# Modulation steps grouped in runs, narrow matmuls gathered around them, and a rearranged entry into the MLP, in a one-core decoder step

## The chip, the cores and the metric

The kernel runs on one core of one Trainium2 chip. The metric is the device time of one execution in microseconds (us), as the median of several runs. The core has a matrix engine (PE, with its weight loads shown as PEld), a vector engine (DVE), an activation engine (ACT), GpSimd (POOL) and a synchronisation engine (SP), which here issues most of the DMA transfers. Each engine executes its own instructions in the order in which they were written to it.

## The reference

One layer of a hybrid decoder runs on a prompt of 256 tokens and on 8 samples of one token each, in fp32, with a model width of 2048:

```python
mod = silu(c) @ w_ada + b_ada                 # 6 x 2048 per sequence
sh1, sc1, gt1, sh2, sc2, gt2 = split(mod, 6)
h = rmsnorm(x, g_pre_mix) * (1 + sc1) + sh1
z = h @ w_in                                  # inputs of three mixers, three gates
y_a = spatial_gating(...)                     # A
y_b = gated_linear_recurrence(...)            # B, 8 heads of 128 x 128
y_c = gated_linear_recurrence(...)            # C, 4 heads of 128 x 256
merged = sum(sigmoid(z_gate[n]) * (y[n] @ w_branch[n]) for n in range(3))
x = x + gt1 * rmsnorm(merged @ w_out, g_post_mix)
h2 = rmsnorm(x, g_pre_mlp) * (1 + sc2) + sh2
x = x + gt2 * rmsnorm(square(relu(h2 @ w_mlp_up)) @ w_mlp_down, g_post_mlp)
```

The recurrent states of prompt and samples, and the normalised rows of mixer A, are outputs as well. `mod` is the **modulation**: six rounds of 2048 values for the prompt and each of the 8 samples.

## The kernel before, in words

**Main work.** All activations stand transposed, 264 columns wide (256 prompt tokens and 8 samples). Every weight tile of 128 x 128 is multiplied three times, with the high and low parts of weights and activations: high x high (L567), high x low (L568), low x high (L569). I call these the main matmuls; there are 13872 of them. A *granule* (`granule`) is 24 of them on one weight block, in two halves of 12. SP loads the raw weights into four buffers, up to five granules ahead (`LOAD_AHEAD`). ACT casts each half to its high part (`whi`, L112), and DVE subtracts to get the low part (`wlo`, L109). Both have six buffers (`SPLIT_BUFS`): the split of a half therefore waits until PE has used the half that stands six before it.

**Stages.** A start with norms and the first two modulation rounds; the mixer inputs (`begin`); the three branches, each with gate and projection matmuls per block of 256 outputs; the output projection `w_out` in eight blocks (m = 0 to 7); a short stretch that I call the *MLP front*; the MLP with eight blocks of up and down projections; a tail.

**Background work.** The mixers are Python generators in the queues `bg` (mixers) and `bs` (samples). After each granule `background` advances them by a rate (`RATES`), and what they emit is thus written between the main matmuls. Three kinds of their PE work use only 32 columns or rows of the array, and I call them **narrow**: levels of the chunked attention (L593, 32 columns), sample reads of the recurrent state (L600) and modulation steps (L307). `slot` emits them together, two levels at most.

**Modulation.** `ada_round` computes rounds 2, 3 and 4 during the branches. A round has 16 steps. A step is four matmuls with 512 moving columns, shown as eight records in the trace. Its two weight tiles `araw` are loaded as soon as the step before it has been issued (L300, two buffers), and steps stand at least four granules apart (`ADA_GAP`). Round 5 has its weights for six steps loaded early into `b` tiles (`N_PRE` = 12 tiles at m = 2 to 5); these steps fill the MLP front, and the other ten run singly in the MLP.

**Waiting places.** `b` tiles (28 buffers) hold most intermediate blocks, and a new one waits for an old one's last reader. The narrow PSUM tiles `sm` have three buffers. In a level, DVE subtracts (L109), ACT takes exponentials (L1077), DVE multiplies twice (L103) and PE reads the result. In the samples, ACT decays the loaded states (L1012) and DVE adds the outer product with a loaded broadcast (`vbc`, L1014). Mixer B and C outputs are transposed back by L1202 and copied by ACT in L1204.

**MLP front.** After the last block of `w_out` come the norm, transposes of the last gated block into the PSUM pair `pt`, sums for the second norm, `residual(q)` (L1466, adds the branch to the residual rows on DVE) and `quad(q)` (L1479 and L1481 scale and transpose four blocks; L1486 and L1488 modulate them). `put_rows(7)` copies `pt` to rows on ACT (L1357) and DVE (L1358). The first MLP accumulators reuse the PSUM that `pt` holds.

Of the kernel before, what the change touches and what calls it, by code (L numbers as in the profile page):

```python
# [15 lines left out]
P = 128  # L16
# [20 lines left out]
RATES = ((1.7, 0.5, 0.27), (1.5, 0.5, 0.27), (1.2, 0.5, 0.27), (1.0, 0.5, 0.27))  # L37
ST_BUFS = 4
VB_BUFS = 2
N_PRE = 12  # L40
PRE_AT = (2, 3, 4, 5)
R0 = 0.3
# [6 lines left out]
FILL = 3  # L49
READY = object()  # L50
SLOT_LATE = 0.9
SLOT_WAIT = 3
# [4 lines left out]
ADA_GAP = 4  # L57
# [3 lines left out]
def hybrid_step_kernel(  # L61
# [229 lines left out]
    def ada_round(r, pre=()):  # L291

        acc = pada.tile([P, 512], F32, tag="ada", name=nm("ada"))

        def load(n):
            if n < len(pre):
                return pre[n]
            w = rawp.tile([P, 1024], F32, tag="araw", name=nm("araw"), bufs=ADA_RAW)
            c0 = r * D + n % 2 * 1024
            nc.sync.dma_start(w, w_ada[0, n // 2 * P:(n // 2 + 1) * P, c0:c0 + 1024])  # L300
            return w

        ws = [load(0), load(1)]
        yield
        for k in range(KT):
            for j in range(4):
                T.matmul(acc[32 * j:32 * j + 32, :], cT[:, k, :], ws[j // 2][:, j % 2 * 512:j % 2 * 512 + 512], start=k == 0, stop=k == KT - 1)  # L307
            ws = [load(2 * k + 2), load(2 * k + 3)] if k + 1 < KT else []
            yield
        am = ada_am(acc, 512)  # L310
        yield
        rows = ada_rows(am, 512)
        ch = slice(r * KT, (r + 1) * KT)
        add(
            mod[:, ch, :].rearrange("p (j i) c -> p i j c", i=4),
            rows[:, :, :, 0:NC],
            badaT[:, ch].rearrange("p (j i) -> p i j", i=4).unsqueeze(3).to_broadcast([P, 4, 4, NC]),
        )
        yield
# [43 lines left out]
    bg, bs, ba = Queue(), Queue(), Queue()  # L363
# [97 lines left out]

    rate = [0.0, 0.0, R0]

# [93 lines left out]
    def granule(w, k0, n, c0, width, accs, xh, xl, k, first, last):  # L557
# [3 lines left out]
        h = n // 2  # L561
        for acc0, m0 in [(acc, 2 * i) for i, acc in enumerate(accs)]:
            for j in range(n):
                for m in range(m0, min(m0 + 2, width // P)):
                    o = acc0[:, m % 2, 0:NT]
                    a, b = (p[:, j % h, m * P:(m + 1) * P] for p in parts[j // h])
                    T.matmul(o, a, xh(k + j), start=first and j == 0, stop=False)  # L567
# [3 lines left out]

    ada_at = [0]

    def ada_due():

        return ba.g and ba.owed >= 0.0 and now[0] >= ada_at[0] + ADA_GAP
# [3 lines left out]
    def slot():  # L580
# [20 lines left out]
        if ada_due():  # L601
            ada_at[0] = now[0]
            ba.step()
# [1054 lines left out]
```

## Time and profile before

| | |
|---|---|
| median of 3 runs | 1972.18 us (1970.73 to 1972.27) |
| the profiled execution's time | 1970.37 us |
| its span in the trace | 1968.6 us, so 1.8 us lie outside |
| mean granted PE clock | 0.994 |
| PE busy | 1919.0 us, 97% |
| DVE busy | 1190.3 us, 60% |
| ACT busy | 1003.6 us, 51% |
| DMA | 442.05 MB, mean 225 GB/s |

A timeline row gives the start of a group of equal instructions, its duration, engine, line, operation, tiles, shape and count. Brackets hold the engine's idle time just before it and what released it. In a table of windows, the third column group gives each engine's busy time in order PE, PEld, DVE, ACT, POOL with record counts, then the granted PE clock as a share of full speed, the DMA share and GB/s. Matmuls overlap, so their distance from start to start matters, not their duration. Line numbers here are those of the kernel before; the changed kernel has about 2 less at the helpers (L109 becomes L107) and about 40 more later (L1202 becomes L1243).

### The profile page before, as it was taken

Reading aid. Unit: us, or ns where it says so; the run is one execution under the profiler, and the core shown is the slowest. Engines: PE = TensorE matmul, PEld = TensorE weight load, DVE = VectorE, ACT = ScalarE, POOL = GpSimd, SP = SyncE. Lnnn points to the kernel's source line nnn. Section 1 sums busy time; section 2 is a strip of 40 time slices with the busy share of each in tenths; the row PEclk is TensorE's granted clock in tenths of the full one; section 3 lists DMA queues with packets and bytes.
Section 4 is the critical chain, followed back from the end, with each engine's and each line's share of the span. In section 5 each row is a group of like instructions: output and inputs, shape, how many; then the busy total and the mean of one; then the engine's idle time right before and its main releaser. Section 6 shows DMA issues by size and latency. Waiting matters only on the chain. (4 is left out here: it accounts for less than half of the span.)

```text
span 1968.6 us, 42184 instructions
## 1 busy us (share of the span) xinstructions
PE 1919.0 (97%) x17008; PEld 1821.4 (93%) x17008; DVE 1190.3 (60%) x2100; ACT 1003.6 (51%) x1818; POOL 83.9 (4%) x142
## 2 busy tenths in 40 slices
PE   6999999999989999999999999999999999999998
PEld 5889999889979999899999989999999999999997
DVE  4566667686766694555555666544555555555665
ACT  5444354655845754644444555444444445454544
POOL 1000000111001111110000000000000000000000
PEclk9999999999999999999999999999999999999999
DMA  9897697788577788678887844767565556566653
GB/s 326 303 337 249 228 302 225 228 252 269 182 240 252 217 265 295 205 251 267 271 249 214 306 141 142 227 220 232 175 182 181 181 179 182 180 181 183 182 178 103
DMA packets 339379, 442.05 MB, mean 225 GB/s; under 512 B 14930, under 2 KB 281024, under 8 KB 339184
## 3 DMA queue, kind: packets, MB, share of 16 engines
q1 hardware_dynamic: 329120, 409.62, 65.5%
q0 software_dynamic: 8992, 28.48, 4.5%
q8 instruction: 133, 2.18, 0.4%
q10 hardware_dynamic: 1072, 1.25, 0.2%
q14 instruction: 62, 0.51, 0.1%
HBM read 427.60 MB, written 11.70 MB: 223 GB/s over the span
## 5 line engine op out<-in xcount | busy, mean ns | idle before, releaser
L567 PE MATMUL mm<-b,whi 128*128 128x264 f32 x4624 | 1330.8, 288 | 10.6 <-ACT b L112 3.5
L568 PE MATMUL mm<-b,whi 128*128 128x264 f32 x4624 | 1318.4, 285 | 1.2 <-DVE b L109 1.2
L569 PE MATMUL mm<-b,wlo 128*128 128x264 f32 x4624 | 1314.3, 284 | 0.0
L109 DVE TENSOR_TENSOR wlo<-raw,whi 128x512 fp32r<-128x512 f32 x1136 | 778.0, 690 | 587.1 <-ACT whi L112 581.5
L112 ACT CAST whi<-raw 128x512 fp32r<-128x512 f32 x1136 | 695.6, 618 | 765.5 <-PE mm L568 681.7
L567 PEld LDWEIGHTS mm<-b,whi 128*128 128x128 f32 x4624 | 872.8, 189 | 70.1 <-ACT whi L112 31.7
L568 PEld LDWEIGHTS mm<-b,whi 128*128 128x128 f32 x4624 | 873.7, 189 | 1.8 <-DVE b L109 1.6
L569 PEld LDWEIGHTS mm<-b,wlo 128*128 128x128 f32 x4624 | 873.2, 189 | 0.0
L106 DVE TENSOR_TENSOR b<-b,mm 128x528 f32<-128x528 f32 (+1 forms) x137 | 95.7, 700 | 44.4 <-PE mm L569 44.4
L1014 DVE SCALAR_TENSOR_TENSOR st<-vbc,b,st 128x128 f32<-128x128 f32 (+1 forms) x96 | 33.8, 392 | 52.0 <-DMA vbc<-vs_d 43.9
L307 PE MATMUL ada<-araw,cT 128*32 128x512 f32 x464 | 63.5, 602 | 0.3 <-DMA araw<-in_w_ada_dram 0.3
L1012 ACT ACTIVATE st<-st,fs 128x128 f32<-128x128 f32 (+1 forms) x96 | 36.8, 430 | 49.3 <-DMA st<-in_state_gla_dram 27.2
L277 PE MATMUL ada<-b,cT 128*32 128x256 f32 (+1 forms) x640 | 35.3, 359 | 6.6 <-ACT b L226 5.6
L103 DVE TENSOR_TENSOR b<-b,b 128x512 f32<-128x512 f32 (+1 forms) x47 | 34.2, 744 | 4.0 <-ACT b L1129 1.4
L277 PEld LDWEIGHTS ada<-b,cT 128*32 128x32 f32 x640 | 18.3, 115 | 18.8 <-ACT b L226 5.6
L1015 POOL DMA_DIRECT2D out_dram<-st x32 | 23.5, 735 | 125.2 <-DVE st L1014 114.5
L109 DVE TENSOR_TENSOR b<-gt,b 128x528 fp32r<-128x528 f32 x32 | 22.7, 709 | 3.7 <-ACT whi L112 0.5
L109 DVE TENSOR_TENSOR b<-b 128x1024 f32<-128x1024 f32 (+1 forms) x21 | 22.4, 1068 | 2.1 <-PE sm L593 1.2
L112 ACT CAST whi<-araw 128x512 fp32r<-128x512 f32 x20 | 12.4, 621 | 21.0 <-PE mm L568 19.2
L103 DVE TENSOR_TENSOR gt<-vt 128x528 f32<-128x528 f32 x32 | 22.5, 702 | 0.9 <-ACT vt L1522 0.9
L1528 ACT ACTIVATE b<-vt 128x528 fp32r<-128x528 f32 x32 | 20.7, 647 | 1.0
L1522 ACT ACTIVATE vt<-mm 128x528 f32<-128x528 f32 x32 | 19.4, 607 | 1.0 <-PE mm L569 1.0
(338 smaller groups left out, 824.2 us busy)
## 6 DMA issues: line engine op xcount, KB each, us to landing
raw<-in_w_in_dram SPq DMA_DIRECT2D x232, 512.0 KB, 4.7
raw<-in_w_mlp_up_dram SPq DMA_DIRECT2D x128, 512.0 KB, 3.9
raw<-in_w_mlp_down_dram SPq DMA_DIRECT2D x128, 512.0 KB, 3.7
araw<-in_w_ada_dram SPq DMA_DIRECT2D x116, 512.0 KB, 5.4
b<-in_w_ada_dram SPq DMA_DIRECT2D x60, 512.0 KB, 7.0
raw<-in_w_branch_dram SPq DMA_DIRECT2D x48, 512.0 KB, 4.9
raw<-in_w_out_dram SPq DMA_DIRECT2D x32, 512.0 KB, 3.9
b<-in_w_ada_dram SPq DMA_DIRECT2D x32, 256.0 KB, 5.8
```

The lines of the kernel that those rows point to most:

```text
L103: V.tensor_tensor(o, a, b, op=ALU.mult)
L106: V.tensor_tensor(o, a, b, op=ALU.add)
L109: V.tensor_tensor(o, a, b, op=ALU.subtract)
L112: S.copy(hi, src)
L277: T.matmul(acc[32 * j:32 * j + 32, 0:n], cT[:, k, :], w[:, n * j:n * j + n], start=k == 0, stop=k == KT - 1)
L307: T.matmul(acc[32 * j:32 * j + 32, :], cT[:, k, :], ws[j // 2][:, j % 2 * 512:j % 2 * 512 + 512], start=k == 0, stop=k == KT - 1)
L567: T.matmul(o, a, xh(k + j), start=first and j == 0, stop=False)
L568: T.matmul(o, a, xl(k + j), start=False, stop=False)
L569: T.matmul(o, b, xh(k + j), start=False, stop=last and j == n - 1)
L1012: S.activation(st[:, i, :], st[:, i, :], AF.Copy, scale=fs[:, h0 + i, b:b + 1])
L1014: V.scalar_tensor_tensor(st[:, i, :], v[:, i, :], k[:, h0 + i, NP + b:NP + b + 1], st[:, i, :], ALU.mult, ALU.add)
L1015: nc.gpsimd.dma_start(G.s_out(b, h0, nh), st)
```

## The change

- `ada_round` becomes a class `Rounds`. Steps collect until a run is full: one at first, two from branch 1, four from the gates of branch 2, two in the MLP. A run is due four granules after its last load (`ADA_LAND`); loads are `pace` granules apart (5, then 4 in branch 2, then 5). The first step of a run loads into `araw`, further ones into `b` tiles. The queue `ba` is gone.
- `background` lets narrow work wait for a due run, up to 4 granules (`SLOT_WAIT`, before 3), and two more for samples of mixer C. The rates of `bg` rise from 1.7, 1.5, 1.2 to 1.8, 1.6, 1.25.
- The decay sums of a recurrence are scanned in place (`c = g`), which saves a `b` tile; the last level then takes its exponent by a subtraction on DVE (three instructions of 128 x 512 in all) ahead of ACT's exponential.
- Mixer A waits one more granule ahead of a transpose (`yield READY`).
- The MLP front: the products on DVE go ahead of the first sum; ACT alone copies the rows of `pt`, right after `d1`; `quad(0)` uses one PSUM tile per block; `residual(0)` moves behind the last granule of `begin_up`; the early loads are four tiles at m = 2, 3 and 4.
- `WIDE`: in block 2 of the MLP's up projection, the first 12 matmuls of each of the four sub-blocks have 272, 288, 320 or 512 moving columns instead of 264. The extra columns of the result are not used.

```diff
+    class Rounds:
...
+        def load(self, place=None):
+            r, k = self.todo.pop(0)
+            ws = []
+            for i in range(2):
+                if place or self.ws:
+                    w = blk([P, 1024])
+                else:
+                    w = rawp.tile([P, 1024], F32, tag="araw", name=nm("araw"), bufs=ADA_RAW)
+                c0 = r * D + i * 1024
+                nc.sync.dma_start(w, w_ada[0, k * P:(k + 1) * P, c0:c0 + 1024])
+                ws.append(w)
+            self.ws.append((r, k, ws))
+            self.at = now[0]
...
+        def due(self):
+            if self.ws:
+                return self.full() and now[0] >= self.at + ADA_LAND
+            return self.done is not None and not self.todo and now[0] >= self.at + 2 * ADA_LAND
...
-        ba.owed = min(ba.owed + rate[2], SLOT_LATE) if ba.g else 0.0
-        wait = max(now[0] + 1 - AGE - min([x[0] for x in levels + samples] + [now[0]]), 0)
-        if ada_due() and (ba.owed >= SLOT_LATE or wait) or wait >= SLOT_WAIT:
+        wait = max([now[0] + 1 - AGE - x[0] for x in levels + samples] + [0])
+        if wait and any(x[1][0].i == 2 for x in samples):
+            wait += 2
+        if rounds.due() and (wait or now[0] >= rounds.at + rounds.pace) or wait >= SLOT_WAIT:
             slot()
+        rounds.tick()
...
-        c = blk()
+        c = g
...
-                S.activation(es, v4(g, 2)[:, :, :, 1:2], AF.Exp)
+                sub(es, cv[:, :, :, 1:2], cv[:, :, :, 0:1])
+                S.activation(es, es, AF.Exp)
...
+        wide = WIDE.get((c0 - 2 * FB, k)) if w.tensor is w_mlp_up.tensor else None
...
+                    if wide and j < 2:
+                        o = acc0[:, m % 2, 0:wide]
...
     quad(0)
     residual(1)
-    put_rows(7, pt, og)
...
+            elif k + 2 == KT:
+                residual(0)
...
-    residual(0)
     pend = up(0, zs)
```

**First place: levels of the second group of mixer B, on DVE.** The PE work that reads `b_7175` stands, in the kernel before, right behind the half that uses `wlo_7170`. These are DVE's rows from that half's split on:

```order
L109 TENSOR_TENSOR wlo_7170<-raw_7058,whi_7169 128x512
L1063 COPY_PREDICATED a_1191_7097<-msk,sm_7181 128x256
L109 TENSOR_TENSOR wlo_7251<-raw_7095,whi_7250 128x512
L109 TENSOR_TENSOR wlo_7255<-raw_7095,whi_7254 128x512
L109 TENSOR_TENSOR wlo_7287<-raw_7137,whi_7286 128x512
L1255 SCALAR_TENSOR_TENSOR b_7023<-gt_7223,mm_7225 128x528
L109 TENSOR_TENSOR wlo_7291<-raw_7137,whi_7290 128x512
L109 TENSOR_TENSOR wlo_7341<-raw_7173,whi_7340 128x512
L109 TENSOR_TENSOR wlo_7345<-raw_7173,whi_7344 128x512
L109 TENSOR_TENSOR b_7175<-b_7007 128x4x256
L103 TENSOR_TENSOR b_7175<-b_7175,b_171 128x4x16x8
L103 TENSOR_TENSOR b_7175<-b_7175,b_6814 128x4x16x8
```

In the changed kernel the same level is `b_7176`, and PE reads it behind the half that uses `wlo_7286`. These are DVE's rows around it:

```order
L107 TENSOR_TENSOR b_7176<-b_173 128x4x256
L107 TENSOR_TENSOR wlo_7086<-raw_6964,whi_7085 128x512
L107 TENSOR_TENSOR wlo_7090<-raw_6964,whi_7089 128x512
L101 TENSOR_TENSOR b_7176<-b_7176,b_171 128x4x16x8
L101 TENSOR_TENSOR b_7176<-b_7176,b_6838 128x4x16x8
L107 TENSOR_TENSOR wlo_7127<-raw_6999,whi_7126 128x512
L1054 SCALAR_TENSOR_TENSOR st_7340<-vbc_7423,b_6838,st_7340 128x128 x2
L107 TENSOR_TENSOR wlo_7131<-raw_6999,whi_7130 128x512
```

Before, six splits stood between the half that PE has just used and the level that it reads next, the last of them in the very buffer that PE has just read; now the level is written many splits ahead of PE's place, and PE reads it later.

**Second place: transposes of mixer C's output, on ACT.** PE's four groups L1202 write `sm_10865`, `sm_10871`, `sm_10877` and `sm_10883` in a row, and ACT copies them; the fourth needs a buffer that the first copy frees. ACT's rows before:

```order
L112 CAST whi_10806<-raw_10669 128x512
L1012 ACTIVATE st_10816<-st_10816,fs_8994 128x256
L112 CAST whi_10810<-raw_10669 128x512
L1012 ACTIVATE st_10816<-st_10816,fs_8994 128x256
L112 CAST whi_10853<-raw_10719 128x512
L1012 ACTIVATE st_10825<-st_10825,fs_8994 128x256 x2
L112 CAST whi_10857<-raw_10719 128x512
L1248 ACTIVATE gt_10888<-mm_10686 128x528
L1204 COPY b_10863<-sm_10865 128x2x256
L1204 COPY b_10863<-sm_10871 128x2x256
L1204 COPY b_10864<-sm_10877 128x2x256
L1204 COPY b_10864<-sm_10883 128x2x256
```

And in the changed kernel, where PE emits three groups and, one granule later, the fourth:

```order
L1052 ACTIVATE st_10560<-st_10560,fs_8974 128x256 x2
L110 CAST whi_10672<-raw_10533 128x512
L110 CAST whi_10676<-raw_10533 128x512
L1245 COPY b_10682<-sm_10684 128x2x256
L1245 COPY b_10682<-sm_10690 128x2x256
L1245 COPY b_10683<-sm_10696 128x2x256
L110 CAST whi_10729<-raw_10596 128x512
L110 CAST whi_10733<-raw_10596 128x512
L1245 COPY b_10683<-sm_10739 128x2x256
```

The state decay L1012 still stands ahead of the copies, but a granule of main matmuls now lies between the third group and the fourth.

**Third place: the MLP front, on DVE.** The rows from `quad(0)` to the next weight splits, before:

```order
L1486 TENSOR_SCALAR vt_15051<-sm_15042,A_14930,mod 128x256
L109 TENSOR_TENSOR b_15036<-vt_15051,b_15032 128x256
L1466 SCALAR_TENSOR_TENSOR b_13653<-b_13665,nr_14960,b_13653 128x512
L109 TENSOR_TENSOR b_15036<-vt_15051,b_15032 128x256
L1486 TENSOR_SCALAR vt_15067<-sm_15058,A_14930,mod 128x256
L1466 SCALAR_TENSOR_TENSOR b_13655<-b_13667,nr_14960,b_13655 128x512
L109 TENSOR_TENSOR b_15036<-vt_15067,b_15032 128x256 x2
L1466 SCALAR_TENSOR_TENSOR b_13653<-b_13665,nr_14960,b_13653 128x512
L1466 SCALAR_TENSOR_TENSOR b_13655<-b_13667,nr_14960,b_13655 128x512
L1358 COPY b_13668<-mm_14969 128x256
L109 TENSOR_TENSOR wlo_15110<-raw_14860,whi_15109 128x512
```

And in the changed kernel:

```order
L1539 TENSOR_SCALAR vt_15041<-sm_15042,A_14931,mod 128x256
L107 TENSOR_TENSOR b_15035<-vt_15041,b_15031 128x256 x2
L1539 TENSOR_SCALAR vt_15058<-sm_15059,A_14931,mod 128x256
L107 TENSOR_TENSOR b_15035<-vt_15058,b_15031 128x256 x2
L1508 SCALAR_TENSOR_TENSOR b_13660<-b_13672,nr_14961,b_13660 128x512
L1508 SCALAR_TENSOR_TENSOR b_13662<-b_13674,nr_14961,b_13662 128x512
L107 TENSOR_TENSOR wlo_15109<-raw_14861,whi_15108 128x512
L107 TENSOR_TENSOR wlo_15113<-raw_14861,whi_15112 128x512
```

Two of the four residual instructions and the copy of `pt` (`mm_14969`) have left the row; the copy now stands on ACT as L1480, behind `d1` and ahead of the second norm.

More of the change, by code (lines that the diff above doesn't have):

```diff
@@ L1408, in hybrid_step_kernel @@
     Q = nc.gpsimd
-    for _ in range(3):
-        next(fill)
+    rounds.steps(2)
     g = gated(7, z, G1)
@@ L1438, in hybrid_step_kernel @@
         S.activation(d1[:, t, :], ident, AF.Copy, scale=r1[:, t:t + 1])
+    for t in range(2):
+        S.copy(in_rows(og, t, 7), pt[:, t])
     xa = tmp([P, KT, NS], "xsn", 1)
```

170 lines of the change are left out of this document (96 added, 74 removed).

## The prediction

> **What bounds the kernel now.** I read the page's totals first, then the busy time by stage, then what PE waits for.
>
> ```profile
> span 1968.6 us, 42184 instructions
> PE 1919.0 (97%) x17008; PEld 1821.4 (93%) x17008; DVE 1190.3 (60%) x2100; ACT 1003.6 (51%) x1818; POOL 83.9 (4%) x142
> L112 ACT CAST whi<-raw 128x512 fp32r<-128x512 f32 x1136 | 695.6, 618 | 765.5 <-PE mm L568 681.7
> ```
>
> PE is busy for 97% of the span, and ACT's casts wait 681.7 us for PE, not the other way round. So time can come only from two places: PE's own instructions, and the roughly 50 us in which PE stands idle. The windows by stage show where the idle time is (before the stages shown, the start has its share, which the change leaves alone):
>
> ```profile
> 560.00:600.00 40.00, 31.79 (x546) 28.88 (x545) 24.56 (x43) 18.56 (x37) 5.37 (x8) 0.91 0.64 202
> 830.00:845.00 15.00, 11.32 (x86) 11.09 (x85) 5.68 (x11) 7.76 (x15) 1.26 (x2) 0.89 0.60 187
> 1166.00:1190.00 24.00, 18.70 (x142) 13.35 (x141) 14.59 (x43) 8.74 (x25) 4.72 (x15) 0.93 0.16 44
> 1190.00:1953.00 763.00, 763.00 (x6265) 753.12 (x6264) 439.13 (x671) 366.86 (x613) 0.00 (x0) 1.00 0.61 185
> ```
>
> The MLP has no idle time at all; three short places lose 8.2, 3.7 and 5.3 us, and there the clock is below 1 as well. PE's timeline shows the single stalls, each with its gap and its releaser:
>
> ```profile
> 350.27 0.33 PE L828 MATMUL sm<-cst,srow 128*128 128x128 f32 x1 [1.75 <-DVE srow L824]
> 570.77 1.08 PE L593 MATMUL sm<-b 128*32 128x32 f32 x64 [3.75 <-DVE b L103]
> 591.23 1.08 PE L593 MATMUL sm<-b 128*32 128x32 f32 x64 [4.46 <-DVE b L103]
> 837.43 1.11 PE L1202 MATMUL sm<-cst,b 128*128 128x128 f32 x4 [3.68 <-ACT b L1204]
> 1185.31 0.56 PE L567 MATMUL mm<-b,whi 128*128 128x264 f32 x1 [3.13 <-DVE b L1358]
> 1188.09 2.06 PE L1479 MATMUL sm<-gt,b 128*128 128x128 f32 x16
> ```
>
> What follows the four long ones is in the windows of 3.4 us around them; the third number from the right, ahead of the DMA share and GB/s, is the granted clock:
>
> ```profile
> 570.50:573.90 3.40, 3.13 (x73) 3.07 (x74) 2.16 (x5) 0.72 (x2) 0.00 (x0) 0.50 0.07 22
> 591.00:594.40 3.40, 3.17 (x80) 2.79 (x81) 1.94 (x5) 1.25 (x2) 1.29 (x2) 0.50 0.40 138
> 836.70:840.15 3.45, 2.71 (x13) 2.72 (x14) 0.43 (x1) 2.24 (x5) 0.00 (x0) 0.51 0.90 307
> 1184.90:1188.30 3.40, 2.99 (x14) 3.02 (x15) 0.95 (x2) 0.81 (x2) 0.00 (x0) 0.50 0.00 0
> ```
>
> The clock is 0.50 for 3.4 us after each, so half of that time, 1.7 us, is lost on top of the gap. A long stall therefore costs 5.45, 6.16, 5.38 and 4.83 us.
>
> **The change part by part: narrow work.** One modulation step stands here between main matmuls, then three steps stand in a row; two more rows give the distance of undisturbed main matmuls, with 28 starts between them:
>
> ```profile
> 1217.11 0.28 PE L569 MATMUL mm<-b,wlo 128*128 128x264 f32 x1
> 1217.33 1.06 PE L307 MATMUL ada<-araw,cT 128*32 128x512 f32 x8
> 1218.32 0.39 PE L567 MATMUL mm<-b,whi 128*128 128x264 f32 x1
> 1218.55 0.29 PE L568 MATMUL mm<-b,whi 128*128 128x264 f32 x1
> ...
> 1172.55 2.78 PE L307 MATMUL ada<-b,cT 128*32 128x512 f32 x24
> ...
> 828.77 0.28 PE L568 MATMUL mm<-b,whi 128*128 128x264 f32 x1
> 832.16 0.29 PE L569 MATMUL mm<-b,wlo 128*128 128x264 f32 x1
> ```
>
> The distance is 3.39 / 28 = 0.121 us. From 1217.11 to 1218.55 are 1.44 us, of which two distances are 0.24: the single step costs 1.20 us. In a row, a further step costs (2.78 - 1.06) / 2 = 0.86. So entering and leaving narrow work costs 0.34 us, whatever its length. In the order of PE's instructions I count 89 separate stretches of narrow work before and 69 after: runs of four in branch 2, runs of two in branch 1 and the MLP, and levels and samples that join them. The instructions are the same in number. 20 x 0.34 = **6.8 us** less, on PE itself and thus on the path.
>
> The price of the gathering is that a level or a sample read may wait one granule longer, two more for mixer C. Behind it wait DVE's masked copies and the mixer's next step, not PE; the raised rates give the mixers back 0.05 to 0.1 of a step per granule. If a mixer were still unfinished when its branch begins, the rest would be drained without cover, as at 837; in the new order no such drain is longer than before, so I take 0.
>
> **The two level stalls.** These rows of DVE and ACT stand ahead of the stalls at 591 and 837, and a subtraction of a level stands between them:
>
> ```profile
> 583.87 1.14 DVE L1014 SCALAR_TENSOR_TENSOR st<-vbc,b,st 128x128 f32<-128x128 f32 x4 [3.78 <-DMA vbc<-vs_d]
> 587.94 1.22 DVE L109 TENSOR_TENSOR b<-b 128x1024 f32<-128x1024 f32 x1
> ...
> 834.99 0.91 ACT L1012 ACTIVATE st<-st,fs 128x256 f32<-128x256 f32 x2 [2.60 <-DMA st<-in_state_gla_dram]
> ```
>
> DVE and ACT execute in order, and both stand 3.78 and 2.60 us before a sample's DMA; splits and the level's products queue behind. PE has six split halves in hand, and such a wait is hidden unless narrow work needs something that stands behind the sixth. The first order excerpt shows that case. In the new order I compared, for each wait of PE, how many splits its producer stands ahead of PE's place: six at exactly the stalls of before, and now six at only two places and four at a third (below). The level products come early enough, so both stalls go: 5.45 + 6.16 = **11.6 us**. The three added subtractions of 128 x 512 cost DVE about half of the 1.22 us of the 128 x 1024 one each, 1.8 us in sum, hidden while DVE is at 60%; uncovered, they would cost that.
>
> **The transposes of mixer C.** The second order excerpt puts a granule (24 x 0.121 = 2.9 us) between the third group and the fourth. A wait on a state's DMA such as the 2.60 us above is then covered: **5.38 us**. Mixer A's extra granule covers the 1.75 us at 350 in the same way: **1.75 us**.
>
> **The MLP front.** The main matmul at 1185.31 waits for the copy of `pt`, which stands behind all residuals:
>
> ```profile
> 1183.42 1.41 DVE L1466 SCALAR_TENSOR_TENSOR b<-b,nr,b 128x512 f32<-128x512 f32 x2
> 1184.74 0.42 DVE L1358 COPY b<-mm 128x256 f32<-128x256 f32 x1
> ```
>
> Now the copy stands on ACT, where it lies in ACT's wait for the second norm, and two residuals are gone from the row. The next thing that is late is `quad(1)`, which needs `residual(1)`: its end at 1184.83 moves up by 1.41 for the two residuals that left, to 1183.4. So `quad(1)` starts at 1183.4 instead of 1188.09, and **4.7 us** are gained; I take 4.5, since `residual(0)` now stands ahead of a later split. If the copies on ACT delay the norm, at most 2 x 0.42 us go back. That `quad(0)` takes a PSUM tile per block, and that the early loads come at three blocks of `w_out` instead of four, I cost at nothing: the tiles free in turn as DVE and ACT read them, and the loads, 4.7 us each, still have two blocks of `w_out` (four granules each, 23 us) to land.
>
> **Late loads.** Two modulation steps waited for their weights:
>
> ```profile
> 257.31 1.78 PE L307 MATMUL ada<-araw,cT 128*32 128x512 f32 x8
> 745.71 1.05 PE L307 MATMUL ada<-araw,cT 128*32 128x512 f32 x4 [0.27 <-DMA araw<-in_w_ada_dram]
> ```
>
> The first lasts 1.78 against 1.06, the second has a gap of 0.27. A run now starts at least four granules, 11.6 us, after its load: **1.0 us** is gained.
>
> **Costs.** `WIDE` adds 12 x (8 + 24 + 56 + 248) = 4032 columns. The trace has no such width on these matmuls. At the rate of the main matmuls, 0.121 / 264 per column, that is **1.85 us**; if the weight load, busy for 753 of the MLP's 763 us, sets the distance, small widths cost nothing, so the bounds are 0 and 1.85, and I take the upper, since the bulk is in the 512 wide ones. [...]
>
> The places with a lead of six or four: sample reads behind ACT's scaling of a state (once new, once as before) and a level in mixer B. The nearest row is a PE wait for an ACT copy at 793 us:
>
> ```profile
> PE sm L1157 <- ACT b L1160: 0.8, 1, 0.8
> ```
>
> Two new waits of that size are **1.6 us**; from below 0, from above a full stall of 6.16 each.
>
> **The sum.** 6.8 + 11.6 + 5.4 + 1.75 + 4.5 + 1.0 = 31.05 gained, 1.85 + 1.6 = 3.45 lost: 27.6 us. From the profiled execution's 1970.4 that gives 1942.8; from the median of 1972.2, 1944.6. I predict 1944.
>
> On the clock, the row is 0.50 after a gap of 3.13 us, so of the 4.83 us at the MLP front 1.7 are clock. [...]
>
> **The rivals.**
>
> *A stall returns elsewhere* (0.18). DVE's and ACT's waits for sample DMAs remain, and where one falls is a matter of a few us:
>
> ```profile
> DVE st L1014 <- DMA vbc<-vs_d: 43.9, 18, 5.5
> ```
>
> 18 such waits, one of 5.5 us. One that meets a place of lead six costs 5.4 to 6.2 instead of 0.8: 1949, or 1955 with two. For it: two such places exist. Against it: five existed before.
>
> *Long narrow runs count as idle for the clock* (0.05). Four runs of four, each about 1.06 + 3 x 0.86 = 3.6 us, would each cost 1.7: 6.8 us, 1951. Against it stands the window with the run of three steps, at full clock:
>
> ```profile
> 1166.00:1181.00 15.00, 12.84 (x106) 7.77 (x105) 8.97 (x33) 5.90 (x18) 4.72 (x15) 1.00 0.26 71
> ```
>
> *The stalls only move* (0.07). If the sample DMAs find another victim each time, only the 6.8 us of narrow work less 1.85 remain: 1967. Against it, the fourth stall (the copy of `pt`) has no DMA in it.
>
> *Slower: SP stands still at modulation loads* (0.03). SP issues raw weights and modulation weights in order:
>
> ```profile
> SPq L300 <- PE ada L307: 93.8, 41, 9.1
> ...
> raw<-in_w_in_dram SPq DMA_DIRECT2D x232, 512.0 KB, 4.7
> ```
>
> Of 41 waits, none over 9.1 us, PE shows no trace: raw weights are issued five granules, 14.5 us, ahead and land in 4.7, which leaves about 9.8. Further steps of a run now load into `b` tiles, and such a load waits for a tile's last reader. If that takes more than about 10 us, PE stalls; with its clock each stall costs about 4.8. In the 13 runs of two or four that would be 62 us: 2007. It decides from six runs on (6 x 4.8 = 29). Against it: the decay sums give a tile back, and most tiles are free long before.
>
> **How the numbers follow.** My forecast has 0.67. The range reaches up to 1956 (two stalls return). Downwards it takes in no new wait and no cost of width (1941), and that two small gaps go too, the 0.8 above and this one, ahead of `quad(0)`:
>
> ```profile
> 1176.75 0.46 PE L1479 MATMUL sm<-gt,b 128*128 128x128 f32 x2 [1.42 <-issue]
> ```
>
> That is 1941.1 - 2.2 = 1938.9, so 1938. The measurement can tell about 0.2%, 3.9 us, from no change. Faster by more: 0.67 + 0.18 + 0.05 and about half of the moved stalls, 0.94; within it: 0.03; slower: 0.03.
>
> **What would show it.** In the changed profile: no gap over 1 us in the windows from 560 to 600 and from 830 to 845, and a clock near 1 there; a main matmul right behind `quad(0)`, and `quad(1)` about 0.5 us after the first granule; runs of four steps that last about 3.6 us without a fall of the clock; the 512 wide matmuls at about 0.23 us. It is wrong if the levels L630 or the copies L1245 show a gap of over 3 us, if SP's wait for `b` tiles lasts over 10 us with PE idle behind it, or if the MLP's PE has gaps.

## The result, and the profile after

| | before | after |
|---|---|---|
| median | 1972.22 us (4 runs) | 1946.30 us (4 runs, 1942.53 to 1946.73) |
| ratio, with 95% interval | | 0.9864 (0.9847 to 0.9881) |
| the profiled execution's time | 1970.37 us | 1945.98 us |
| its span | 1968.6 us | 1944.2 us |

The change is worth 25.9 us by the medians and 24.4 us by the two profiled executions; 1944 was forecast. The totals of the changed kernel's page, which answer to those shown of before:

```profile
span 1944.2 us, 42159 instructions
PE 1907.4 (98%) x17008; PEld 1818.1 (94%) x17008; DVE 1188.3 (61%) x2102; ACT 1005.0 (52%) x1819; POOL 83.7 (4%) x142
```

PE is busy for 11.6 us less with the same number of instructions, and stands idle for 12.8 us less. Now the windows of the changed kernel around the places that stood out before (the numbers behind the counts are the granted clock, the DMA share and GB/s), and one over all branches and the MLP:

```profile
560.00:600.00 40.00, 38.69 (x624) 35.79 (x623) 29.57 (x55) 23.28 (x48) 6.12 (x9) 1.00 0.82 264
815.00:845.00 30.00, 27.98 (x227) 26.12 (x227) 16.74 (x31) 15.67 (x31) 6.70 (x10) 1.00 0.95 339
1146.00:1170.00 24.00, 22.39 (x183) 17.10 (x182) 15.89 (x45) 12.80 (x32) 4.97 (x15) 1.00 0.24 67
240.00:1928.00 1688.00, 1681.60 (x14913) 1617.20 (x14913) 1044.32 (x1814) 893.05 (x1625) 77.68 (x126) 1.00 0.69 219
```

The clock is 1.00 throughout; of the 8.2, 3.7 and 5.3 us of idle time 1.3, 2.0 and 1.6 are left. What remains of PE's waits in the branches, from the timeline of the changed kernel:

```profile
592.05 0.39 PE L610 MATMUL mm<-b,whi 128*128 128x264 f32 x1 [1.26 <-issue]
...
708.57 0.28 PE L612 MATMUL mm<-b,wlo 128*128 128x264 f32 x1 [1.27 <-issue]
...
822.73 0.40 PE L612 MATMUL mm<-b,wlo 128*128 128x264 f32 x1 [0.98 <-DVE wlo L107]
...
840.30 0.39 PE L612 MATMUL mm<-b,wlo 128*128 128x264 f32 x1 [1.04 <-DVE wlo L107]
```

Four new gaps of about 1 us, none at a place that I had named; the clock stays at 1.00 behind all four. A run of four modulation steps, of the changed kernel too:

```profile
880.35 1.07 PE L343 MATMUL ada<-araw,cT 128*32 128x512 f32 x8
881.24 2.76 PE L343 MATMUL ada<-b,cT 128*32 128x512 f32 x24
883.92 0.39 PE L610 MATMUL mm<-b,whi 128*128 128x264 f32 x1
884.15 0.28 PE L611 MATMUL mm<-b,whi 128*128 128x264 f32 x1
```

From 880.35 to the next main matmul are 3.57 us, where a single step took 1218.32 - 1217.33 = 0.99: three further steps cost 0.86 each, as in the row of three of before.

### The profile page after: what moved, and what is told of

Its sections match the earlier page's. It is cut to its first block, busy times and chain, and to the rows that moved or that the text cites. A ratio compares the mean times of both kernels' runs of the same rounds, so it can differ in the third digit from the quotient of the medians.

```text
span 1944.2 us, 42159 instructions
## 1 busy us (share of the span) xinstructions
PE 1907.4 (98%) x17008; PEld 1818.1 (94%) x17008; DVE 1188.3 (61%) x2102; ACT 1005.0 (52%) x1819; POOL 83.7 (4%) x142
## 3 DMA queue, kind: packets, MB, share of 16 engines
q8 instruction: 133, 2.18, 0.4%
q10 hardware_dynamic: 1072, 1.25, 0.2%
## 4 chain that ended last, share of the span: by engine, by line
PE 95%; DMA 3%; DVE 1%; ACT 1%; issue 1%; POOL 0%; SPq 0%; DVEq 0%; ACTq 0%; POOLq 0%
PE mm L610 29%; PE mm L611 28%; PE mm L612 28%; PE ada L343 3%; PE ada L275 1%; DMA vbc<-vs_d 1%; PE sm L777 1%; PE sm L630 1%; DMA b<-in_w_ada_dram 1%; PE sm L1157 1%; DMA raw<-in_w_in_dram 1%; PE sm L637 0%; DMA b<-in_x_prompt_dram 0%; PE sm L1527 0%; DVE wlo L107 0%
## 5 line engine op out<-in xcount | busy, mean ns | idle before, releaser
L610 PEld LDWEIGHTS mm<-b,whi 128*128 128x128 f32 x4608 | 868.1, 188 | 51.6 <-issue 30.3
L343 PE MATMUL ada<-araw,cT 128*32 128x512 f32 x296 | 39.4, 600 | 0.0
L343 PE MATMUL ada<-b,cT 128*32 128x512 f32 x216 | 26.2, 594 | 0.0
L107 DVE TENSOR_TENSOR b<-b 128x1024 f32<-128x1024 f32 (+1 forms) x24 | 24.4, 1020 | 0.0
L110 ACT CAST whi<-araw 128x512 fp32r<-128x512 f32 x20 | 12.5, 623 | 19.4 <-PE mm L611 17.5
```

Source lines behind the costliest of these rows:

```text
L107: V.tensor_tensor(o, a, b, op=ALU.subtract)
L110: S.copy(hi, src)
L343: T.matmul(self.acc[32 * j:32 * j + 32, :], cT[:, k, :], ws[j // 2][:, j % 2 * 512:j % 2 * 512 + 512], start=k == 0, stop=k == KT - 1)
```

## The experiments

**Theory A:** a long stall needs a producer that stands six split halves ahead of PE's place, and a sample's transfer that is late in front of it; whoever changes the position removes the stall and the fall of the clock behind it. **Rival B:** the late transfers make the stalls, and they find another victim. **Rival C:** a narrow stretch costs nothing by itself. The kernel before ran beside each group on the same chip, with medians of 1973.7 to 1975.1 us, so ratios are compared.

**1. Decay sums in place, alone.**

```diff
-        c = blk()
+        c = g
...
-                S.activation(es, v4(g, 2)[:, :, :, 1:2], AF.Exp)
+                sub(es, cv[:, :, :, 1:2], cv[:, :, :, 0:1])
+                S.activation(es, es, AF.Exp)
```

> The kernel before, with the decay sums scanned in place and the last level's exponent from a subtraction, nothing else. Theory A (a stall needs a producer that stands six splits ahead of PE's place, and a late sample transfer in front of it): the new order takes the two levels of mixer B's second group out of that position, so the gaps near 571 and 591 us (3.75 and 4.46) fall below 1 us and the clock stays at 1.0 there; the stalls at 350, 837 and 1185 us stay; time 1972.2 - 11.6 = about 1961. Theory B (the late transfers alone make the stalls, and they find another victim): gaps of 3 us or more appear elsewhere in the same stage, time 1969 to 1973.

Measured: ratio 0.9965 (0.9953 to 0.9977), 6.9 us less. The stage's window of this kernel, and its gaps:

```profile
560.00:600.00 40.00, 38.63 (x650) 35.21 (x638) 27.65 (x52) 20.53 (x42) 5.38 (x8) 1.00 0.82 263
```

```profile
553.76 0.39 PE L569 MATMUL mm<-b,wlo 128*128 128x264 f32 x1 [1.14 <-DVE wlo L109]
...
556.63 0.39 PE L569 MATMUL mm<-b,wlo 128*128 128x264 f32 x1 [1.15 <-DVE wlo L109]
...
575.11 0.28 PE L567 MATMUL mm<-b,whi 128*128 128x264 f32 x1 [1.37 <-issue]
...
832.54 0.47 PE L1203 MATMUL sm<-cst,b 128*128 128x128 f32 x1 [4.58 <-ACT b L1205]
```

Both level stalls and their clock windows are gone by this edit alone, 11.6 us. DVE's wait for a sample ahead of the second one is still there, 3.92 us instead of 3.78, and no stall stands behind it:

```profile
584.11 1.14 DVE L1014 SCALAR_TENSOR_TENSOR st<-vbc,b,st 128x128 f32<-128x128 f32 x4 [3.92 <-DMA vbc<-vs_d]
```

Three gaps of 1.1 to 1.4 us come in their place, and the stall of the transposes is 0.9 longer, as ACT's wait for a state in front of it is 0.8 longer (3.42 against 2.60); the MLP front's stall, untouched, cost two windows of the clock in this profile, not one. 11.6 - 3.7 - 0.9 - 1.7 = 5.3, where this profiled execution took 1969.9 and the kernel before had a median of 1975.1 on the chip. The position is what makes the long stall; of the 11.6 us, a third comes back in small gaps. So A holds for the position, and B for a part of the sum. Whether the late transfer is needed too is the question of experiment 5.

**2. The copies at the MLP front put back behind quad and residual**, in the changed kernel.

```diff
-    for t in range(2):
-        S.copy(in_rows(og, t, 7), pt[:, t])
...
     quad(0)
     residual(1)
+    put_rows(7, pt, og)
```

> The changed kernel, with the copies of the last rows at the MLP front put back behind the quad and the residual (half on ACT, half on DVE). Theory A: PE's main matmul waits again for DVE's copy; the two residuals in front of it are gone, so the gap is about 3.1 - 1.4 = 1.7 us, too short for the clock to fall, part of which replaces the 0.1 us wait of the next quad; time about 1.5 us above the changed kernel, 1948. Rival: the copy was only late because of the clock and the order around it, and nothing is lost: 1946.

Measured: ratio 0.9885 (0.9868 to 0.9901). The kernel of experiment 4 ran beside it at 1945.23; with the 1.8 us of its narrower matmuls added, this one's 1950.82 is 3.8 us above the changed kernel, not 1.5. The gap and the clock behind it:

```profile
1163.04 0.39 PE L610 MATMUL mm<-b,whi 128*128 128x264 f32 x1 [2.21 <-DVE b L1401]
```

```profile
1164.10:1167.50 3.40, 3.40 (x18) 3.40 (x17) 1.90 (x3) 1.10 (x2) 0.00 (x0) 0.50 0.03 4
```

The gap is 2.21 us and the clock is 0.50 for 3.4 us after it: 2.21 + 1.7 = 3.9. I had expected a gap of 1.7 us with the clock at 1.00 behind it, as behind the 1.75 us at 350 in the kernel before.

**3. Every modulation step by itself**, in the changed kernel.

```diff
-    rounds.batch = 2
...
-    rounds.pace, rounds.batch = 4, 4
+    rounds.pace = 4
...
-    rounds.pace, rounds.batch = 5, 2
+    rounds.pace = 5
```

> The changed kernel with every modulation step by itself (runs of one throughout, same pace). 88 narrow stretches instead of 69. Theory A: 19 x 0.34 = 6.5 us more, 1953. Rival C (a stretch costs nothing by itself, the gain is only in the stalls): no more than 1 us, 1946 to 1947. With single steps the second load of a run no longer needs a b tile, so waits of DVE for the samples' broadcast of over 6 us should be fewer if the paired loads caused them.

Measured: ratio 0.9916 (0.9901 to 0.9931), 1958.04 us, 11.0 above the changed kernel as reckoned for this chip (1945.23 + 1.8). The order of the mixers' work moved too, and a stall came back:

```profile
807.37 0.33 PE L1243 MATMUL sm<-cst,b 128*128 128x128 f32 x1 [2.40 <-ACT b L1234]
```

```profile
808.00:814.80 6.80, 6.22 (x31) 3.32 (x30) 3.55 (x6) 3.51 (x8) 2.71 (x4) 0.50 0.72 235
593.00:596.40 3.40, 3.40 (x18) 3.40 (x17) 1.90 (x5) 2.92 (x7) 0.99 (x2) 0.50 0.90 282
```

Half a clock over 6.8 and 3.4 us is 5.1 us. The gaps add up to the same 30.3 us as in the changed kernel. By the spans (1957.2, against 1944.3 + 1.8) 11.1 - 5.1 = 6.0 us are left for 19 more stretches: 0.32 us each, against 0.34 in the prediction. Rival C falls. That paired loads cause the long broadcast waits can't be read from this run, since the order moved.

**4. No wider matmuls**, in the changed kernel.

```diff
-WIDE = {(0, 0): 272, (CW, 0): 288, (2 * CW, 0): 320, (3 * CW, 0): 512}
+WIDE = {}
```

> The changed kernel without the wider matmuls (all 264 columns). From the distances in its trace (272: 0.125, 288: 0.132, 320: 0.147, 512: 0.232 against 0.121 us) the 48 wide ones cost 1.8 us: 1944.5. Rival: the widened stretch is hidden or helps something behind it: 1946. Also a second look at the changed kernel's four new gaps of 1.0 to 1.3 us near 590, 707, 821 and 839 us: theory (they come from late sample transfers and from instruction issue, by chance) says they move or change size; if they are set by the order they stand at the same places.

Measured: ratio 0.9852 (0.9838 to 0.9867) beside 0.9864 of the changed kernel; the 1.8 us lie within the intervals, so the price is read from the trace (below). The four gaps stand at the same places:

```profile
593.76 0.39 PE L610 MATMUL mm<-b,whi 128*128 128x264 f32 x1 [1.46 <-issue]
...
710.34 0.29 PE L612 MATMUL mm<-b,wlo 128*128 128x264 f32 x1 [1.33 <-issue]
...
824.47 0.39 PE L612 MATMUL mm<-b,wlo 128*128 128x264 f32 x1 [0.88 <-DVE wlo L107]
...
842.36 0.39 PE L612 MATMUL mm<-b,wlo 128*128 128x264 f32 x1 [1.05 <-DVE wlo L107]
```

Experiment 2, with the same order in the branches, has them there too (1.24, 1.37, 0.82 and 1.04 us). They are not chance: the order of the work sets them. A fifth, of 0.90 us at 429, is new in this one.

**5 and 6. Transfers of the samples used five granules after their issue**, in the kernel before, and in that of experiment 4.

```diff
-FETCHED = 3
+FETCHED = 5
```

> The kernel before with one number changed: a sample's states and broadcast are used five granules after their loads are issued instead of three. PE's critical producers still stand six splits ahead at the places of before. Theory A (both are needed, the position and a late transfer): ACT's and DVE's waits for these transfers nearly vanish, and with them the long gaps near 571, 591 and 837 us, each to below 1.5 us and without a fall of the clock: 1972.2 - 17.0 + 3 x 0.8 = about 1958. Rival D (the position alone makes the stall): gaps of 3 us and more stay at these places, 1970 to 1974.

> The changed kernel without the wider matmuls, and with the samples' transfers used five granules after their issue. Theory: the two gaps of 1.0 us behind late low parts of weights near 821 and 839 us come from DVE's waits of up to 8 us for the samples' broadcast, which now vanish: 2 us less than the changed kernel without wide matmuls (1945.2), so about 1943, and a ratio to the kernel before of 0.984. The gaps of 1.3 us near 592 and 709 us that have no releaser stay, since they have nothing to do with the samples. Rival: new positions six splits ahead (three of them now) cost as much as is won: 1945.

Measured: ratios 1.0035 (1.0021 to 1.0048) and 0.9952 (0.9938 to 0.9967), both slower than what they started from, by 7 and about 20 us. DVE's wait for the broadcast in experiment 5 (in all, times, longest), where the kernel before had 43.9 in 18:

```profile
DVE st L1014 <- DMA vbc<-vs_d: 54.2, 19, 4.1
```

And a stall of experiment 6 in the timeline:

```profile
683.77 0.48 PE L1256 MATMUL sm<-cst,os 128*128 128x128 f32 x1 [12.52 <-ACT os L1066]
```

The edit didn't do all that I wanted: DVE's waits are not shorter in sum, and the samples' chain was stretched, until the branch that needs its sums waited 12.5 us (experiment 6). But near the level stalls the waits did go: between 551 and 594 us of experiment 5 neither DVE nor ACT waits for a sample's transfer, and the stalls at 571 and 591 us stayed (3.75 and 3.78). DVE's rows ahead of the second, and PE's:

```profile
586.49 0.69 DVE L109 TENSOR_TENSOR wlo<-raw,whi 128x512 fp32r<-128x512 f32 x1 [0.77 <-ACT whi L112]
587.10 1.22 DVE L109 TENSOR_TENSOR b<-b 128x1024 f32<-128x1024 f32 x1
589.05 1.29 DVE L103 TENSOR_TENSOR b<-b,b 128x512 f32<-128x512 f32 x2 [0.73 <-ACT b L1077]
...
590.40 0.73 PE L593 MATMUL sm<-b 128*32 128x32 f32 x62 [3.78 <-DVE b L103]
```

The sixth split waits for ACT's cast, which waits for PE to free the buffer; behind it the level's own subtraction, exponential and products take from 587.10 to 590.34, and the level is PE's next instruction. The kernel before shows the same at 571: DVE's last wait for a sample ended at 550.47 there. So for the levels the position alone is enough, as the rival had it, and A's second condition is wrong.

**7. The old pace of the mixers and of narrow work**, in the changed kernel.

```diff
-RATES = ((1.8, 0.5), (1.6, 0.5), (1.25, 0.5), (1.0, 0.5))
+RATES = ((1.7, 0.5), (1.5, 0.5), (1.2, 0.5), (1.0, 0.5))
...
-SLOT_WAIT = 4
+SLOT_WAIT = 3
...
-        if wait and any(x[1][0].i == 2 for x in samples):
-            wait += 2
```

> The changed kernel with the old rates of the mixers (1.7, 1.5, 1.2), narrow work waiting for three granules as before, and without the two extra granules for mixer C's samples. The transposes of mixer C's output stand again as 16 in one drain, with a copy six splits ahead. Theory A: the stall near 837 us returns if a state's transfer is late there, with 2.5 to 4.5 us and the clock's 1.7: 1950 to 1953; the levels of mixer B stay free of stalls. Rival B: 1946, nothing hangs on these numbers.

Measured: 1950.45 us, ratio 0.9873 (0.9856 to 0.9889). The transposes of mixer C stall again, and the clock falls for two windows:

```profile
826.68 0.47 PE L1241 MATMUL sm<-cst,b 128*128 128x128 f32 x1 [2.28 <-ACT b L1243]
```

```profile
825.80:832.60 6.80, 5.92 (x30) 3.47 (x31) 1.58 (x3) 2.96 (x6) 2.99 (x5) 0.50 0.80 245
```

The new pace is what separates the fourth group of transposes from the third, as A has it. The two gaps behind late low parts are missing here, which gives part of it back; the ratio is that of the changed kernel within the intervals, so the stall is shown by the trace, not by the time.

**8. A ladder of idle stretches in the MLP**, in the kernel of experiment 4.

```diff
+LADDER = (1, 2, 3, 4, 5, 6, 8)
...
             S.activation(rl, z, AF.Relu)
+            if f:
+                lad = tmp([P, P], "os0", 1)
+                for _ in range(LADDER[f - 1]):
+                    nc.gpsimd.tensor_copy(lad, rl[:, 0, 0:P])
+                T.transpose(sm([P, P]), lad, ident)
```

> The changed kernel without wide matmuls, and with 28 idle stretches put into PE's MLP: behind four up blocks of each of blocks 1 to 7 PE waits for 1, 2, 3, 4, 5, 6 or 8 copies on GpSimd and then transposes a scratch tile; the result is not used. From the runs so far (no fall of the clock after 1.75 us, a fall after 2.21, 3.13 and more): stretches up to 1.7 us cost only themselves, and from 2.2 us on each also costs 1.7 us of a clock at 0.50 for 3.4 us. [...]

Measured: one run, 2079.8 us. It has four gaps of each size: 1.46, 2.18, 2.99, 3.34, 3.70, 4.05 and 4.77 us. Three rows of its timeline that the sizes alone don't explain:

```profile
1339.07 0.33 PE L1581 MATMUL sm<-cst,os 128*128 128x128 f32 x1 [2.17 <-POOL os L1580]
...
1369.90 0.33 PE L1581 MATMUL sm<-cst,os 128*128 128x128 f32 x1 [2.18 <-POOL os L1580]
...
1577.99 0.33 PE L1581 MATMUL sm<-cst,os 128*128 128x128 f32 x1 [3.34 <-POOL os L1580]
```

The windows behind these three (the third number from the right is the clock):

```profile
1339.10:1342.50 3.40, 3.40 (x28) 3.40 (x29) 1.25 (x2) 0.86 (x2) 0.00 (x0) 1.00 0.52 159
1370.50:1373.90 3.40, 3.40 (x21) 3.40 (x21) 0.70 (x2) 0.62 (x1) 0.00 (x0) 0.63 0.39 129
...
1578.00:1581.40 3.40, 3.40 (x28) 3.40 (x29) 0.69 (x1) 0.85 (x2) 0.00 (x0) 1.00 0.30 104
```

None of the four gaps of 1.46 us lets the clock fall, one of the four of 2.18, three of the four of 3.34, and all sixteen of the other sizes. So a gap of 3.34 us kept its clock here and one of 2.18 lost it: no bound on the length of a gap, mine at 2.2 us included, says what happens. What the falls of this run have in common is in the last section.

**9 and 10. The MLP front alone, and three parts together**, in the kernel before. The first takes the change's edits at the front and nothing else; the second adds the decay sums in place and mixer A's extra granule, with pace and modulation as before.

> The kernel before with only the MLP front of the changed one (products ahead of the first sum, the copies of the last rows on ACT, one PSUM tile per block of the first quad, the first residual moved behind the eighth granule). Theory: the gap of 3.1 us ahead of the second granule half goes, with the 3.4 us at a clock of 0.50 behind it, and the second quad starts about 4.7 us earlier; nothing else moves, so the time falls by 4.5 to 5.4 us, ratio 0.9975. Rival: the copies on ACT delay the second norm and half of it is lost, 2 to 3 us.

> The kernel before with three parts together: decay sums in place, the MLP front, and mixer A's extra granule ahead of its transpose; modulation and narrow work are paced as before (91 narrow stretches). If parts add: 6.9 (decay sums alone, measured) + 4.8 (front) + 1.75 = 13.5 us less, ratio 0.993; the sixteen transposes in one drain stay and keep a stall of 3 to 5 us there. Theory B (stalls move with every shift of the order): the extra granule shifts all of the mixers' work by one granule, new gaps of 2 us and more appear in the branches, and the sum is 8 us or less.

Measured: 0.9971 (0.9959 to 0.9983), 5.7 us less, for the front; 0.9946 (0.9928 to 0.9964), 10.7 us less, for the three. Parts that measured 6.9 and 5.7, with 1.75 expected of the granule, make 14.35. The intervals, each of some 2 us and more to either side, would allow that they add; the trace of experiment 10 shows a loss that neither part has alone. Its timelines, PE first and then ACT:

```profile
706.08 0.59 PE L567 MATMUL mm<-b,whi 128*128 128x264 f32 x1 [3.87 <-ACT whi L112]
```

```profile
703.58 0.51 ACT L1013 ACTIVATE st<-st,fs 128x256 f32<-128x256 f32 x1 [7.20 <-DMA st<-in_state_gla_dram]
```

ACT stood 7.2 us before a state's transfer, long enough to use up all the split halves that PE had in hand; here no position was needed. With the clock at 0.50 for two windows behind it the stall cost 3.9 + 3.4 = 7.3 us. The order had moved, and a long wait for a transfer met PE at a new place. That is rival B, in one place.

**11. No modulation loads in branch 1**, in the kernel of experiment 4. The steps of that branch multiply a constant that is in place, so part of the modulation is left out.

```diff
             r, k = self.todo.pop(0)
+            if self.batch == 2 and place is None and r < 5:
+                self.ws.append((r, k, None))
+                self.at = now[0]
+                return
...
+                    w = cst[:, 256:768] if ws is None else ws[j // 2][:, j % 2 * 512:j % 2 * 512 + 512]
```

> The changed kernel without wide matmuls, where the modulation steps of branch 1 are computed from a constant that is in place already: eight to ten steps lose their loads of 1 MB each, so part of the modulation is left out. Theory (the loads of a run, issued close together, delay the transfers of the samples): DVE's waits for the samples' broadcast, 8.1 us at the longest, fall below 5, the two gaps of 1.0 us behind late low parts of weights near 824 and 842 us go, and the time is 2 us below the kernel without wide matmuls, ratio 0.984. Rival: the samples' transfers are late by their own latency and their place; waits and gaps stay, ratio 0.985. The gaps of 1.3 us without a releaser near 594 and 710 us stay by both.

Measured: 1939.71 us, ratio 0.9827 (0.9812 to 0.9842) against 0.9852 (0.9838 to 0.9867) for experiment 4, by the middles 5 us, though the intervals just meet. The later part of the branch in the windows of experiment 4, then of this kernel (the second number is PE's busy time, the one ahead of the last the DMA share):

```profile
700.00:850.00 150.00, 146.54 (x1477) 135.27 (x1476) 88.43 (x162) 82.75 (x169) 28.63 (x43) 1.00 0.84 277
```

```profile
700.00:850.00 150.00, 149.85 (x1511) 139.31 (x1511) 91.56 (x166) 84.48 (x172) 28.92 (x44) 1.00 0.73 230
```

PE's idle time falls from 3.46 to 0.15 us. The gaps near 824 and 842 are gone, and so is the one near 710; that near 594 stays at 1.33. By the trace the loads did cost, 3.3 us here and more than the 2 expected, and one of the gaps without a releaser went with them. DVE's waits for the broadcast are 43.7 us instead of 51.4, the longest 7.3 instead of 8.8 and not below 5: most of that wait lies elsewhere.

**12. Branch 1 without modulation steps**, all of the computation done: experiment 4 with the steps of branch 1 moved to runs of four behind it.

```diff
-            if self.todo and not self.full() and now[0] >= self.at + self.pace:
-                self.load()
+            if self.batch != 2 or self.todo[0:1] and self.todo[0][0] == 5:
+              if self.todo and not self.full() and now[0] >= self.at + self.pace:
+                  self.load()
...
-    rounds.pace, rounds.batch = 4, 4
+    rounds.pace, rounds.batch = 3, 4
```

> A version that should beat both kernels: no wider matmuls, no modulation steps in branch 1 (where mixer C's samples load their states), and the steps left over as runs of four in branch 2 and the output projection, three granules between loads instead of four; all of the computation is done. 71 narrow stretches instead of 69. Theory (modulation loads delay the samples' transfers and PE's instructions in branch 1): the gaps near 710, 824 and 842 us of the kernel without wide matmuls go, 4.4 us as in the run without these loads, less 2 x 0.34: 1945.2 - 3.7 = about 1941.5, ratio 0.983. Rival: the loads only collide with raw weights later, or two new places six splits ahead cost as much: 1945, ratio 0.985, with new gaps in branch 2.

Measured: 1944.53 us (1942.30 to 1945.90), ratio 0.9851 (0.9834 to 0.9867). The same window of this kernel:

```profile
700.00:850.00 150.00, 149.03 (x1442) 142.23 (x1441) 94.76 (x180) 87.55 (x180) 28.10 (x42) 1.00 0.75 243
```

The gaps near 710, 824 and 842 us are gone here as well, a new one of 0.97 stands at 762, and the idle time in the window is 0.97 instead of 3.46. Yet the ratios of this kernel and of experiment 4 are the same within their intervals, so no gain over experiment 4 is shown; both beat the kernel before.

## Why the prediction was right

**Narrow stretches, 6.8 us:** right. A further step of a run takes 0.86 us, and 19 stretches fewer are worth about 6.0 us (experiment 3).

**Level stalls, 11.6 us:** right in the position, shown by experiment 1, and wrong in the cause that I put beside it, the wait for a sample's DMA. DVE's timeline has the rows of the first excerpt in their written order, from the masked copy at 558.07 to the level's subtraction at 567.50 and its products at 569.42. What I left out is the short gaps: the four of the changed kernel are 4.55 us, where I had counted 1.6 at other places. Two of them (0.98 and 1.04) are lateness that comes back, behind waits of DVE for samples (2.72 us up to 821.19, 3.55 up to 839.16); the other two have no releaser in the profile (last section). The sign that I had named, no gap over 1 us in these windows, was missed by the gaps at 592 and 840. At the two places with a lead of six PE's timeline shows no wait worth the name. My sentence that such positions are "exactly the stalls of before" said too much: the order before has two more of them, in front of transposes of the gated outputs, where PE did not stall. Experiment 1 shows that the position is needed for these stalls: the wait of DVE stayed, and the stalls went. Experiment 5 and the stall at 571 of the kernel before show that it is enough: there is no late transfer ahead of them. The late transfer can have added at most the 0.7 us by which the stall of 4.46 exceeds the others. The sum was right all the same, because the change takes away the position and not the transfers.

**Mixer C's transposes, 5.38, and the 1.75 at 350 us:** both gone. Experiment 7 brings the first back with the old pace. Here a late transfer does lengthen the stall (experiment 1).

**MLP front, 4.5 us:** 5.0 in the trace. The last main matmul of the branches and the 33rd behind it, of the kernel before and of the changed one:

```profile
1166.79 0.29 PE L569 MATMUL mm<-b,wlo 128*128 128x264 f32 x1
...
1190.96 0.28 PE L569 MATMUL mm<-b,wlo 128*128 128x264 f32 x1
```

```profile
1146.73 0.28 PE L612 MATMUL mm<-b,wlo 128*128 128x264 f32 x1
...
1165.86 0.28 PE L612 MATMUL mm<-b,wlo 128*128 128x264 f32 x1
```

That is 24.17 us before and 19.13 after. Alone the edit measured 5.7 us, with an interval of 3.4 to 8.1 (experiment 9).

**Late loads, 1.0:** no step waits for its weights any more; the page gives 0.0 us of idle time ahead of L343.

**Width, 1.85 us:** 12 matmuls of each width stand 0.125, 0.132, 0.147 and 0.232 us apart, against 0.121: 12 x (0.004 + 0.011 + 0.026 + 0.111) = 1.8. The upper bound was right; the weight loads hid none of these 1.8 us. These are the first and the last row of the widest twelve and the next main matmul:

```profile
1352.18 0.40 PE L606 MATMUL mm<-b,whi 128*128 128x512 f32 x1
...
1354.73 0.39 PE L608 MATMUL mm<-b,wlo 128*128 128x512 f32 x1
1354.96 0.28 PE L610 MATMUL mm<-b,whi 128*128 128x264 f32 x1
```

**The sum.** 31.05 - 3.45 = 27.6 was forecast, 24.4 came out between the profiled executions. 3.2 us are missing. The new gaps cost 4.55 - 1.6 = 2.95 more than counted; the start, which the change leaves alone, was 1.3 us slower in this execution (the 501st main matmul starts at 115.56 against 114.23); the front gave 0.5 more. 2.95 + 1.3 - 0.5 = 3.75, and the half us beyond 3.2 is within the terms. The 0.8 us by which experiment 3 puts the narrow stretches lower is made up by the wait of 0.82 at 794, which went as well.

**The rivals.** A returned stall didn't happen in full, but the two gaps behind late low parts are its small form. Long runs of narrow work cost no clock: it is 1.00 through the runs of four steps, that of 3.57 us at 880.35 among them. SP's waits didn't reach PE as a stall of its own, yet the modulation loads do reach it another way: without them PE's idle time between 700 and 850 us was 0.15 us instead of 3.46, and DVE's waits for the samples' broadcast 43.7 instead of 51.4 (experiment 11); I had looked only at the queue, not at what the loads share with the others.

## What to carry to other kernels

Ask of every instruction that the bottleneck engine waits for how far ahead of it its producer stands in the producer's own order; where that distance uses up all the buffers between them, the producer's own chain shows in full (3.75 us here without any late transfer), and a late transfer in its queue comes on top. Count a stall of 3 us with the slow clock behind it, which here mostly cost 1.7 us, and 3.4 in experiments 1, 7 and 10. And expect no part of such a change to add up exactly: each edit moves the rest of the order, and some of the lateness finds another place.

## What the hardware showed that was not expected

**The falls of the clock start on one grid, behind windows with much idle time.** In the kernel before, the five falls between 100 and 1200 us start at 106.28, 570.50, 590.98, 836.73 and 1184.89, and the last four lie 136, 142, 214 and 316 times 3.413 us behind the first. All falls of the ladder (experiment 8) start on one grid of 3.413 us too: 1371.4, 1446.5, 1463.5, 1480.6, 1497.7 and so on, to 0.01 us. Each lasts one window of it, or two. I laid this grid over PE's gaps in the MLP of that kernel. Every window with up to 1.82 us of idle time is followed by the full clock, every one with 1.93 us or more by a fall; only where the clock is down already, a second window falls with less as well (0.9 to 1.5 in three cases of four). That fits the three rows: the gap at 1339 puts 1.82 us into one window, that at 1370 1.93, and the gap of 3.34 at 1578 lies across two, with 1.53 and 1.82. The kernel before fits (1.64 without, 2.72 and more with a fall), experiments 1 and 9 too (1.74 without; 1.88 with). In stretches with narrow work it doesn't hold as sharply: windows with gaps of 1.30 (experiment 5), 1.45 (experiment 7), 1.66 (experiment 3) and 1.78 us (the ladder's own branches, at 825) were followed by a fall, and what counts as idle there is open.

**Gaps without a releaser stand at one place in PE's instruction stream.** If PE's records of the trace are counted (matmuls, weight loads and the sequencer's) and divided into blocks of 256, the pair behind each of the 21 such gaps in the branches (0.14 to 1.99 us, in eleven kernels) is at number 193 or 194 of a block: 11458 and 13761 in the changed kernel, 10689 in experiment 1, 7618 in 6, 11201 and 14530 in 7. The 256 records ahead of such a gap go by in 1.5 to 5.6 us, because narrow work is dense in them, where main matmuls alone take 15.5 us for as many. (The gap of 1.42 us without a releaser at the MLP front of the kernel before stands at 148 and is none of these.) The page's instruction queue has 133 packets with 2.18 MB, 16 KB each, and PE's 34175 records in the changed kernel make 133 full blocks:

```profile
q8 instruction: 133, 2.18, 0.4%
```

The traces have the times of these packets. Ahead of each of the 21 gaps a packet of this queue lands 1.26 to 1.54 us before the matmul that ends the gap (at 590.51 and 707.30 in the changed kernel, for the matmuls at 592.05 and 708.57). At no such place in the fourteen kernels, from 200 us on, does PE go on less than 1.22 us behind its packet, and where the packet landed more than 1.54 us ahead there is no gap; in the MLP it lands 13 us and more ahead. The packet ahead of a gap starts 0.7 to 3.9 us after PE has passed the place before. From these times I take it that PE stood waiting for the packet; that is an estimate, and no run tested it by itself. What delays the packet is open: in experiment 11, without the loads, it started 1.34 us behind that place instead of 2.68, and the gap near 710 was gone.
